# Sums of weight quarters in HBM: 32 transfers of 512 KB instead of 16 of 1 MB, from attention on

## The chip, the cores and the metric

The kernel runs on one core of a Trainium2 chip. TensorE does the matrix products, VectorE (DVE) and ScalarE (ACT) the elementwise work and the splitting of operands, GpSimd (POOL) a little arithmetic and the DMAs of its own queue, SyncE (SP) issues nearly all loads. The metric is the device time of one execution in microseconds (us), lower is better. Runs of before: 1167.38, 1168.90 and 1169.53 us, median 1168.9.

## The reference: two layers of attention, convolution and SwiGLU

Input is 512 tokens of 1024 features, float32. Each of two layers does:

```python
h = rms_norm(x, pre_mix_norm[l])
proj = h @ w_in[l]                                # q | k | v | conv_u | gate_b | gate_c
attn = dilated_mixture_attention(rope(q), rope(k), v)       # 8 heads, three dilated windows
conv_y = gate_b * short_conv(gate_c * conv_u, conv_w[l])    # depthwise, width 3
merged = concat(rms_norm(attn), rms_norm(conv_y))
x = x + rms_norm(merged @ w_out[l], post_mix_norm[l])
h = rms_norm(x, pre_ffn_norm[l])
g, u = split(h @ w_gate_up[l])                    # 2 x 2816 columns
f = (silu(g) * u) @ w_down[l]                     # 2816 -> 1024
x = x + rms_norm(f, post_ffn_norm[l])
```

## The kernel before

**Operands in two parts.** Every float32 operand is split into a rounded high part and the rest, and a product is three matmuls: high x high, high x low, low x high (mm3, lines 250 to 252). ScalarE makes the high part (line 221 for a weight half of 128 x 1024, 820 in the seven-product stage), VectorE the low part (222, 821).

**Weights.** A layer's weights lie in HBM in chunks of 1 MB, two halves of 512 KB each. load_raw (line 122) loads a half into one of three buffers, raw; a load waits until VectorE has read the buffer's last contents. split_half asks for the next two halves before it splits one. SP issues all of this in program order, so a wait at one load holds whatever stands behind it. The order of TensorE and SP is that of the program (a manual schedule); that of the other engines is made by the scheduler, and GpSimd's sum instructions are kept in the program's order among themselves.

**A layer's stages, in TensorE's order.** (1) in_proj_attention: projections, with attention's steps and the rotary and convolution work advanced between them; advance() is called once per weight tile of eight, 66 times a layer. (2) out_proj. Meanwhile split_by_dma makes the high and low parts of the first gate/up chunk by DMA on GpSimd's queue: a load (line 233), a negated copy on ScalarE (234), an accumulating load on top of it (235). (3) feed_forward: the gate/up product in 22 chunks. Chunks 0 to 3 are done directly, three of them in two halves of the tokens. Chunks 4 to 21 (the loop on SEVEN) are done in Strassen's manner, seven products of quarters instead of eight, which needs sums of weight quarters; prepare() makes these on chip, one chunk ahead: line 837 reads the chunk's first raw half, 838 its second too, 840 and 845 make the rest. The matmuls stand at line 900, 84 a chunk, of 256 columns. Line 777 multiplies gate and up. (4) The down projection: again seven products of quarters (line 994), in the order of weight_source: product 0 takes a quarter of the down weights as it is, product 1 the sum t1, then t2, a quarter, t3, a quarter, t4. A product takes four halves of 512 KB. The rest of the rows goes directly (line 1056).

**The sums in memory.** t1 to t4 are sums of the down weights' quarters, 2 MB each, made by DMA within HBM into tsum, one tensor a layer. weight_sums(l) is a generator; each step issues one transfer on GpSimd's queue, and the feed-forward stage takes a step behind every seven-product chunk. Six rounds: t1 and t3 are copies of a quarter; t1 and t3 each get another quarter added (an accumulating DMA, which reads its destination too); t2 is a copy of t1, then gets a quarter added; t4 is a copy of t2, then gets one added. Before, a transfer is 2048 columns of 128 rows, 1 MB, so that there are 16 a layer, behind chunks 4 to 19; eight are plain and eight accumulate.

**The token.** What sets a transfer's time is a token: SP issues a DMA of one number into a small buffer (due, line 158), behind the loads that the program has issued so far; GpSimd copies it (seen, line 159), so it waits until the token has landed; the transfer (line 160) follows. In the seven-product stage the token stands behind the two loads that prepare() issued for the next chunk but one.

Of the kernel before, what the change touches and what calls it, by code (L numbers as in the profile page):

```python
# [36 lines left out]
KS = 8  # L37
# [45 lines left out]
def encoder(ctx: ExitStack, tc: tile.TileContext, x, xT, pos, mask, cols, rows, w, wd, out):  # L83
    nc = tc.nc
# [6 lines left out]
    def nm(base):  # L91
        uid[0] += 1
        return f"{base}_{uid[0]}"

    def big(shape, dt=F32):
        return sb.tile(shape, dt, tag="big", bufs=11, name=nm("big"))
# [10 lines left out]
    def small(n, dt=F32):  # L107
        return sb.tile([P, n], dt, tag="small", bufs=24, name=nm("small"))

    def bank(tag):  # L110
        return ps.tile([P, 512], F32, tag=tag, bufs={"acc": 4, "att": 3, "pv": 1}[tag], name=nm(tag))
# [15 lines left out]
    def down_quarter(l, g, f):  # L127

        c = (2 * g + f) * KS * 512
        return wd[l][:, c:c + KS * 512]  # L130
# [15 lines left out]
    def weight_sums(l):  # L146

        b11, b12, b21, b22 = (down_quarter(l, g, f) for g in range(2) for f in range(2))  # L150
        t1, t2, t3, t4 = (tsum[l][:, k, :] for k in range(4))
        for pairs in (((t1, b11), (t3, b12)), ((t1, b12), (t3, b22)), ((t2, t1),), ((t2, b22),), ((t4, t2),), ((t4, b21),)):
            for n, (o, src) in enumerate(pairs):
                for c in range(0, KS * 512, 2048):
                    add = {"accum_op": ALU.add} if src is b22 or src is b21 or (src is b12 and o is t1) else {}
                    due = small(1)[:1]
                    seen = sb.tile([1, 1], F32, tag="seen", bufs=2, name=nm("seen"))
                    nc.sync.dma_start(due, cols[0:1, 0, 0:1])
                    tc.keep_in_program_order(nc.gpsimd.tensor_copy(seen, due))
                    tc.keep_in_program_order(nc.gpsimd.dma_start(o[:, c:c + 2048], src[:, c:c + 2048], **add))  # L160
                    yield

    tc.keep_in_program_order(nc.scalar.preload_act_table_set("trig_and_small"))
# [74 lines left out]
    def take(n, h, keep=None):  # L238


        return take_half(2 * n + h, keep)
# [7 lines left out]
    def mm3(o, sh, sl, mh, ml, start, stop):  # L249
        nc.tensor.matmul(o, sh, mh, start=start, stop=False)  # L250
        nc.tensor.matmul(o, sh, ml, start=False, stop=False)  # L251
        nc.tensor.matmul(o, sl, mh, start=False, stop=stop)  # L252
# [44 lines left out]
    def transposed(t, h, hT, tag, raw=None):  # L297
        for g in range(2):
            b = bank(tag)
            for k in range(4):  # L300
                nc.tensor.transpose(b[:, k * P:(k + 1) * P], h[:, (4 * g + k) * P:(4 * g + k + 1) * P], ident)
            b4 = b.rearrange("p (k t) -> p k t", k=4)
            hi = hT[0][g][:, :, t * P:(t + 1) * P]
            lo = hT[1][g][:, :, t * P:(t + 1) * P]
            nc.scalar.copy(hi, b4)
            nc.vector.tensor_sub(lo, b4, hi.bitcast(F32))
            if raw is not None:
                nc.scalar.copy(raw[g][:, :, t * P:(t + 1) * P], b4)
# [12 lines left out]
    def pair_full(n, hT, step=None, tag="acc"):  # L321
        accs = [bank(tag), bank(tag)]
        pair_part(n, accs, hT, 0, S, step)
        return accs
# [121 lines left out]
    def run_background(n=None):  # L446

        while background and n != 0:
            try:
                next(background[0])  # L450
                n = None if n is None else n - 1
            except StopIteration:
                background.pop(0)
# [143 lines left out]
                nc.scalar.activation(V[:, t, :], accs[t], AF.Copy, scale=inv[:, 2 * t:2 * t + 1])  # L597
        return inv

    def in_proj_attention(l, hT, h, tables):  # L600

        base = l * NCHUNK
        V = big([P, NT, S])
        accs = [None] * NT

        def values(t, g, turn=None):
            if accs[t] is None:
                accs[t] = bank("acc")
            for kt in range(4 * g, 4 * g + 4):
                if turn is not None and kt == 4 + TURN // 2:  # L610
                    transposed(turn, h[turn], hT, "acc")
                hi, lo = take(base + g, (kt % 4) // 2, 2 * base if t < NT - 1 else None)
                c = (kt % 2) * 512
                mm3(accs[t], hT[0][g][:, kt % 4, t * P:(t + 1) * P], hT[1][g][:, kt % 4, t * P:(t + 1) * P],
                    hi[:, c:c + 512], lo[:, c:c + 512], kt == 0, kt == KT - 1)
            if g == 1:
                nc.scalar.copy(V[:, t, :], accs[t])

        inv = None
        if l == 0:  # L620
            inv = first_values(hT, V)
            nc.sync.dma_start(mask_sb, mask)
        else:
            for o in [(0, 0), (0, 1, 2), (1, 0), (1, 1, 3), (2, 0), (2, 1), (3, 0), (3, 1)]:
                values(*o)

        qks = [None] * 4
        merged = [None] * 4
        sq_a = sb.tile([P, S], F32, tag="sqa", bufs=1, name=nm("sqa"))
        sq_c = sb.tile([P, S], F32, tag="sqc", bufs=1, name=nm("sqc"))  # L630
        att = attention(l, qks, V, merged, sq_a)
        count = [0]

        def advance():
            for _ in range(PACE[count[0] % len(PACE)]):
                next(att, None)
            run_background(BG)
            count[0] += 1

        made = []  # L640
        for j in range(4):
            if j == 1:
                merged[0:2] = [big([P, 2, 2, S], F32R) for _ in range(2)]
            seen = [0]

            def step():
                seen[0] += 1
                if l == 0 and j == 0 and seen[0] == TURN_ROT:
                    made.extend(rotary_tables(*angles, inv))
                if j > 1 or (j == 1 and seen[0] > START):  # L650
                    advance()
                elif j == 1:
                    run_background(BG)

            accs = pair_full(base + 2 + j, hT, step, "att" if l == 0 and j == 0 else "acc")
            if l == 0 and j == 0:
                tables, scaled, inv2 = made
            qk = big([P, 4, S], F32R)
            kl = sb.tile([P, 2, S], F32R, tag="kl", bufs=2, name=nm("kl"))
            background.append(rope_split(accs, scaled if l == 0 else tables, qk, kl))  # L660
            qks[j] = (qk, kl)
        merged[2:4] = [big([P, 2, 2, S], F32R) for _ in range(2)]
        kinds = ["u", "c", "b"] * 4
        held = {}
        for n in range(6):
            accs = pair_full(base + 6 + n, hT, advance)
            for m in range(2):
                i, kind = divmod(2 * n + m, 3)
                kind = "ucb"[kind]
                if kind == "u":  # L670
                    t = sb.tile([P, S], F32, tag="u", bufs=1, name=nm("u"))
                    if l == 0:
                        nc.vector.tensor_mul(t, accs[m], inv2)
                    else:
                        nc.scalar.copy(t, accs[m])
                    held["u", i] = t
                else:
                    held[kind, i] = accs[m]
                if kind == "b":
                    background.append(conv_tile(i, held["u", i], held["b", i], held["c", i], merged, l, sq_c))  # L680
        for _ in att:
            pass
        run_background()
        return merged, sq_a, sq_c, tables, inv
# [58 lines left out]
    def feed_forward(l, hT, hs, raw, adding):  # L743
# [35 lines left out]
        def gated_full(m, accs):  # L779
            sg = tmp([P, S])  # L780
            nc.scalar.activation(sg, accs[0], AF.Silu)
            gated(m, sg, accs[1])
# [159 lines left out]
        for m in range(3):  # L942
            pair_part(base + m, accs[m], hT, HS, S, step, keep if m == 0 else None)
            gated_full(m, accs[m])
        ahead = None
        for m in range(3, SEVEN):
            n = [0]
# [29 lines left out]
        hT = None  # L977
        hs = [None] * NT
# [64 lines left out]
        for f in range(2):  # L1043
            if f == 1 and gnext is not None:
                hT = new_hT()
            for t in range(NT):
                for m in range(2 * KS, MT):
# [5 lines left out]
                    c = (j % 2) * 512  # L1053
# [17 lines left out]
    with tc.manual_schedule(engines={mybir.EngineType.PE, mybir.EngineType.SP}):  # L1071
        warm_up()
        hs = [None] * NT
        hT = new_hT()
        tables = None
        for l in range(DEPTH):
            adding = weight_sums(l)
            merged, sq_a, sq_c, tables, inv = in_proj_attention(l, hT, hs, tables)
            hT, hs, raw = out_proj(l, merged, sq_a, sq_c, inv)
            hT, hs = feed_forward(l, hT, hs, raw, adding)  # L1080

# [87 lines left out]
```

## Time and profile before

| what | value |
|---|---|
| runs, median | 1168.9 us (1167.38 to 1169.53) |
| profiled execution | 1170.38 us, span 1168.4 us |
| granted TensorE clock | 0.997 |
| seven-product stage, layer 0 / layer 1 | 284.98 to 468.69 / 865.02 to 1051.61 us |
| DMA share, 285 to 470 us / 30 to 230 us | 0.69 / 0.29 |
| sums' DMAs, issued | 292.1 to 450.1 and 872.0 to 1031.2 us |
| HBM traffic | 159.36 MB read, 35.65 MB written |

The page's groups give line, engine, operation, the tiles (out<-in), their shape, the count, busy time and the mean of one. A row of a timeline gives start and duration in us, the engine, the line, and in brackets how long the engine stood before it and what ended that. "Waits" sum such times by who waited for whom. The chain follows the work that ended last back to its releasers. TensorE's matmuls overlap, so that one's duration is longer than the distance from one start to the next. A DMA row on POOL or SP is the issue; its landing is given apart. Rows by stretch give the length, the busy times of TensorE, its weight loads, VectorE, ScalarE and GpSimd with their counts, the granted clock, the share of the DMA engines and GB/s.

### The profile page before, as it was taken

How to read it: one execution, taken by the hardware profiler on the slowest of the kernel's cores; microseconds unless marked ns; L12 is line 12 of the kernel's file. 1: busy time of each engine (PE TensorE's matmuls, PEld its weight loads, DVE VectorE, ACT ScalarE, POOL GpSimd, SP SyncE). 2: the span in 40 equal slices, each digit the busy share in tenths (PEclk: the TensorE clock that was granted, in tenths of full speed). 3: DMA queues.
4: the chain of work that ended last, by engine and by line, in shares of the span. 5: the costliest groups of instructions: out<-in, count | busy, mean ns of one | idle time of the engine just before them, and what ended most of it. 6: DMA issues, size and time to landing. Idle time of an engine off the chain costs nothing.

```text
span 1168.4 us, 18250 instructions
## 1 busy us (share of the span) xinstructions
PE 1148.5 (98%) x7008; PEld 1010.5 (86%) x7008; DVE 841.4 (72%) x1392; ACT 669.8 (57%) x1263; POOL 70.0 (6%) x127
## 2 busy tenths in 40 slices
PE   9999999999999999999999999999999999999997
PEld 8777778899999999888777777788999999998886
DVE  5798664776886778984757986448767777789844
ACT  7577544564655656663545775446545556567632
POOL 6000011000010000000000000110000011000000
PEclk9999999999999999999999999999999999999999
DMA  8221234222677777665223212441136776676641
GB/s 323 91 72 55 73 90 126 74 73 90 206 185 191 213 216 181 217 203 176 69 66 100 73 55 72 126 125 53 59 125 193 203 196 182 207 181 213 198 144 73
DMA packets 41911, 162.64 MB, mean 139 GB/s; under 512 B 4960, under 2 KB 4960, under 8 KB 37728
## 3 DMA queue, kind: packets, MB, share of 16 engines
q1 hardware_dynamic: 35344, 122.64, 32.8%
q0 software_dynamic: 5760, 37.75, 13.7%
q8 instruction: 55, 0.90, 0.3%
q10 hardware_dynamic: 720, 1.09, 0.3%
q14 instruction: 32, 0.26, 0.1%
HBM read 159.36 MB, written 35.65 MB: 167 GB/s over the span
## 4 chain that ended last, share of the span: by engine, by line
PE 44%; DVE 3%; DMA 2%; ACT 1%; issue 1%; DVEq 0%; ACTq 0%; SPq 0%
PE acc L900 7%; PE att L900 6%; PE acc L250 5%; PE acc L251 5%; PE acc L252 5%; PE acc L994 5%; PE att L994 2%; DMA raw<-in_w 2%; PE acc L1056 1%; PE pv L487 1%; PE att L480 1%; PE att L1056 1%; PE att L250 1%; PE att L252 1%; PE att L251 1%
## 5 line engine op out<-in xcount | busy, mean ns | idle before, releaser
L222 DVE TENSOR_TENSOR wl<-raw,wh 128x1024 fp32r<-128x1024 f32 x140 | 170.7, 1220 | 79.3 <-ACT wh L221 78.2
L900 PE MATMUL acc<-big,wh 128*128 128x256 f32 x1152 | 212.2, 283 | 0.0
L221 ACT CAST wh<-raw 128x1024 fp32r<-128x1024 f32 x140 | 146.9, 1051 | 108.8 <-PE acc L251 35.9
L900 PEld LDWEIGHTS acc<-big,wh 128*128 128x128 f32 x1152 | 179.8, 192 | 0.2
L900 PE MATMUL acc<-big,wl 128*128 128x256 f32 x576 | 163.7, 284 | 2.8 <-DVE wl L821 2.8
L900 PE MATMUL att<-big,wh 128*128 128x256 f32 x864 | 160.7, 283 | 0.2 <-ACT att L908 0.2
L250 PE MATMUL acc<-big,wh 128*128 128x512 f32 (+1 forms) x400 | 154.0, 385 | 0.0
L252 PE MATMUL acc<-big,wl 128*128 128x512 f32 (+1 forms) x400 | 149.5, 374 | 0.0
L251 PE MATMUL acc<-big,wh 128*128 128x512 f32 (+1 forms) x400 | 149.3, 373 | 0.0
L900 PEld LDWEIGHTS att<-big,wh 128*128 128x128 f32 x864 | 134.6, 192 | 0.5 <-ACT att L908 0.4
L900 PE MATMUL att<-big,wl 128*128 128x256 f32 x432 | 123.2, 285 | 0.4
L820 ACT CAST wh<-t 128x512 fp32r<-128x512 f32 x144 | 88.7, 619 | 45.8 <-PE att L900 30.7
L900 PEld LDWEIGHTS acc<-big,wl 128*128 128x128 f32 x576 | 110.5, 192 | 3.9 <-DVE wl L821 3.7
L821 DVE TENSOR_TENSOR wl<-t,wh 128x1024 fp32r<-128x1024 f32 x72 | 87.7, 1218 | 17.3 <-ACT wh L820 17.3
L994 PE MATMUL acc<-wh,big 128*128 128x512 f32 x320 | 99.5, 389 | 0.0
L820 ACT CAST wh<-raw 128x512 fp32r<-128x512 f32 x108 | 63.4, 619 | 47.0 <-PE acc L900 31.3
L252 PEld LDWEIGHTS acc<-big,wl 128*128 128x128 f32 x400 | 75.3, 188 | 13.9
L250 PEld LDWEIGHTS acc<-big,wh 128*128 128x128 f32 x400 | 75.4, 189 | 12.3 <-issue 0.8
L251 PEld LDWEIGHTS acc<-big,wh 128*128 128x128 f32 x400 | 75.6, 189 | 11.6
L900 PEld LDWEIGHTS att<-big,wl 128*128 128x128 f32 x432 | 82.8, 192 | 2.2 <-DVE wl L821 2.2
L821 DVE TENSOR_TENSOR wl<-raw,wh 128x512 fp32r<-128x512 f32 x72 | 68.5, 951 | 6.2 <-ACT wh L820 6.0
L994 PEld LDWEIGHTS acc<-wh,big 128*128 128x128 f32 x320 | 60.1, 188 | 12.4
(265 smaller groups left out, 2225.5 us busy)
## 6 DMA issues: line engine op xcount, KB each, us to landing
raw<-in_w SPq DMA_DIRECT2D x144, 512.0 KB
tsum<-in_wd POOLq DMA_DIRECT2D x24, 1024.0 KB, 8.1
raw<-in_wd SPq DMA_DIRECT2D x36, 512.0 KB
raw<-tsum SPq DMA_DIRECT2D x32, 512.0 KB
tsum<-tsum POOLq DMA_DIRECT2D x8, 1024.0 KB, 5.3
gain<-in_rows SPq DMA_DIRECT2D x7, 512.0 KB
big<-in_xT SPq DMA_DIRECT2D x8, 256.0 KB
raw<-in_w SPq DMA_DIRECT2D x8, 256.0 KB
```

The lines of the kernel that those rows point to most:

```text
L221: nc.scalar.copy(hi, raws[i])
L222: nc.vector.tensor_sub(lo, raws[i], hi.bitcast(F32))
L250: nc.tensor.matmul(o, sh, mh, start=start, stop=False)
L251: nc.tensor.matmul(o, sh, ml, start=False, stop=False)
L252: nc.tensor.matmul(o, sl, mh, start=False, stop=stop)
L480: nc.tensor.transpose(tp[:, k * P:(k + 1) * P], sm[:, k * P:(k + 1) * P], ident)
L487: nc.tensor.matmul(o[hd * 64:hd * 64 + 64, half * 256:half * 256 + 256], V[:, k, hc:hc + 64], PT[hd][:, k, :], start=k == 0, stop=k == NT - 1)
L820: nc.scalar.copy(hi[:, c:c + 512], src[:, c:c + 512])
L821: nc.vector.tensor_sub(lo[:, :n], src[:, :n], hi[:, :n].bitcast(F32))
L900: nc.tensor.matmul(o[:, :HS], sh[:, c], mh[:, k, :], start=start and k == 0 and n == 0, stop=k == 3 and n == 2, skip_group_check=True)
L994: nc.tensor.matmul(outs[i], sh[:, k, st], mh[:, c:c + 512], start=start and k == 0 and n == 0, stop=False, skip_group_check=True)
L1056: nc.tensor.matmul(accs[f][t], sh[:, t * P:(t + 1) * P], mh[:, c:c + 512], start=False, stop=m == MT - 1 and n == 2, skip_group_check=True)
```

## The change

A transfer of the sums is 1024 columns, 512 KB, so a layer has 32, in the same six rounds. The generator is handed to in_proj_attention too. There every sixth call of advance() takes a step (calls 6, 12, ... of 66: 11 steps); each of the first three gate/up chunks takes one behind its second half (3 steps); each seven-product chunk takes one as before (18 steps, 4 to 21). 11 + 3 + 18 = 32, so that none is left for the loop behind the stage. By kind: the plain copies are transfers 1 to 8, 17 to 20 and 25 to 28, the accumulating ones 9 to 16, 21 to 24 and 29 to 32.

```diff
@@ weight_sums @@
-                for c in range(0, KS * 512, 2048):
+                for c in range(0, KS * 512, 1024):
...
                     nc.sync.dma_start(due, cols[0:1, 0, 0:1])
                     tc.keep_in_program_order(nc.gpsimd.tensor_copy(seen, due))
-                    tc.keep_in_program_order(nc.gpsimd.dma_start(o[:, c:c + 2048], src[:, c:c + 2048], **add))
+                    tc.keep_in_program_order(nc.gpsimd.dma_start(o[:, c:c + 1024], src[:, c:c + 1024], **add))
                     yield
@@ in_proj_attention @@
-    def in_proj_attention(l, hT, h, tables):
+    def in_proj_attention(l, hT, h, tables, adding):
...
         def advance():
+            if count[0] % 6 == 5:
+                next(adding, None)
             for _ in range(PACE[count[0] % len(PACE)]):
                 next(att, None)
             run_background(BG)
@@ feed_forward @@
         for m in range(3):
             pair_part(base + m, accs[m], hT, HS, S, step, keep if m == 0 else None)
             gated_full(m, accs[m])
+            next(adding, None)
@@ encoder @@
-            merged, sq_a, sq_c, tables, inv = in_proj_attention(l, hT, hs, tables)
+            merged, sq_a, sq_c, tables, inv = in_proj_attention(l, hT, hs, tables, adding)
```

## The prediction, made before the result was known

> **What bounds the kernel now.** I read the page first, then the stretches where TensorE changes stage, then the gaps inside the stage that the sums share with the weight loads, then what those gaps wait for. The page says that TensorE is busy almost all the time, so only its own gaps can be won; and it lists the sums, which GpSimd's queue q0 issues (packets, MB, share of the 16 engines' span).
>
> ```profile
> PE 1148.5 (98%) x7008; PEld 1010.5 (86%) x7008; DVE 841.4 (72%) x1392; ACT 669.8 (57%) x1263; POOL 70.0 (6%) x127
> ...
> q0 software_dynamic: 5760, 37.75, 13.7%
> ...
> tsum<-in_wd POOLq DMA_DIRECT2D x24, 1024.0 KB, 8.1
> ```
>
> In before all 16 sums of a layer run in the seven-product stage (line 900). How long is that stage, and how long need it be? TensorE's timeline gives its first matmul and the first one of the down projection (line 994) for layer 0; the chain gives the start for layer 1, and its own step.
>
> ```profile
> 284.98 0.40 PE L900 MATMUL acc<-big,wh 128*128 128x256 f32 x2
> ...
> 468.69 0.40 PE L994 MATMUL acc<-wh,big 128*128 128x512 f32 x1
> ...
> 865.02 2.87 PE acc L900 x24
> ...
> 895.25 2.88 PE acc L900 x24
> 898.13 1.44 PE att L900 x12
> ...
> 1051.61 0.40 PE L994 MATMUL acc<-wh,big 128*128 128x512 f32 x1
> ```
>
> 24 matmuls take 2.88 us undisturbed, 0.12 us each. The code issues 18 chunks x 7 products x 12 matmuls = 1512, so 181.44 us. Layer 0 took 468.69 - 284.98 = 183.71 us, layer 1 took 1051.61 - 865.02 = 186.59 us: 2.27 and 5.15 us lost, **7.4 us** together. That is all that this stage can give back. The chain names the cause for one of the gaps: a weight load that lands late, then VectorE's work on it (838), then the low half of a split (821) that TensorE stands for.
>
> ```profile
> 994.76 6.37 DMA raw<-in_w
> ...
> 1001.22 0.69 DVE t L838
> ...
> 1004.31 1.15 DVE wl L821
> ```
>
> ```profile
> 1003.77 0.38 PE L900 MATMUL acc<-big,wl 128*128 128x256 f32 x1 [0.88 <-DVE wl L821]
> ```
>
> So the lateness is that of the loads. Is it due to the sums? VectorE's timeline answers, by line 837, the first operation that needs a chunk's first load: beside the plain copies that open the stage it waits for nothing, from the first accumulating sum on it does, and late in the stage by 3.57 us.
>
> ```profile
> 302.20 0.69 DVE L837 TENSOR_TENSOR t<-raw 128x512 f32<-128x512 f32 x1
> ...
> 342.91 0.69 DVE L837 TENSOR_TENSOR t<-raw 128x512 f32<-128x512 f32 x1 [0.43 <-DMA raw<-in_w]
> ...
> 999.99 0.69 DVE L837 TENSOR_TENSOR t<-raw 128x512 f32<-128x512 f32 x1 [3.57 <-DMA raw<-in_w]
> ```
>
> The waits of the stage put a sum on it, layer 0 and layer 1 (us, times, longest):
>
> ```profile
> DVE t L837 <- DMA raw<-in_w: 16.0, 10, 3.0
> ...
> DVE t L837 <- DMA raw<-in_w: 18.4, 9, 3.6
> ```
>
> The sums' own rows, asked for by stretch, agree. First the four plain copies of layer 0 (290 to 332 us), then the four accumulating ones behind them (330 to 372 us), and last the two 512 KB accumulating DMAs of line 235, the nearest thing in this trace to a sum of the new size (the landing time there is that of these and of two plain 512 KB loads).
>
> ```profile
> L160 POOL DMA_DIRECT2D tsum<-in_wd x4: 515/524/587, 292.1 to 323.2; - x4
> ...
> DMA to landing us min/median/max: 4.9/5.1/5.3
> ...
> L160 POOL DMA_DIRECT2D tsum<-in_wd x4: 826/837/855, 333.7 to 366.8; - x4
> ...
> DMA to landing us min/median/max: 8.0/8.2/8.8
> ...
> L235 POOL DMA_DIRECT2D big<-in_w x2: 877/884/891, 182.1 to 762.0; - x2
> ...
> DMA to landing us min/median/max: 4.1/5.0/6.2
> ```
>
> Plain 1 MB: 5.1 us. Accumulating 1 MB: 8.2 us, and VectorE is late. Beside a plain one (302 to 313 us) the row of that stretch, its length and then the busy times with TensorE first, shows no gap:
>
> ```profile
> 302.00:313.00 11.00, 11.00 (x94) 11.00 (x93) 8.99 (x13) 6.37 (x14) 1.03 (x3) 1.00 0.66 197
> ```
>
> VectorE's slack takes up the first late loads; TensorE's gaps come in the stage's second half.
>
> **The change in the seven-product stage.** TensorE's, ScalarE's and VectorE's orders stay as they are (but for one pair of neighbours on VectorE); what moves is DMA traffic, SP's tokens and GpSimd's issues. Each chunk now carries 512 KB of sum, not 1 MB, and all 18 chunks carry one. A sum's place within the chunk's 10.08 us (84 x 0.12) stays:
>
> ```profile
> 302.87 0.53 POOL L160 DMA_DIRECT2D tsum<-in_wd  x1
> ...
> 306.19 3.42 SPq L122 DMA_DIRECT2D raw<-in_w  x2
> ```
>
> The sum starts 3.3 us ahead of the next chunk's first load. A sum of 8.2 us overlaps that load for 4.9 us and makes it late; one of 5.1 us overlaps for 1.8 us and does not. For a 512 KB sum I bound the landing by half of 8.2 (4.1 us) and by 6.2, the slowest of the 512 KB row, and take 5.0, its median: overlap 1.7 us, so like the plain copies, no gap. **Term: -7.4 us, less 0.2** for small gaps that hang on VectorE's order alone (an estimate: two of 0.1 us). At 6.2 us the overlap is 2.9, 1.1 of the 3.1 us between no wait and the full one: a third of the loss, 2.6 us, would stay. The Trainium skill ("DMA: Bandwidth & Descriptors", section "Anatomy of one DMA") has a fixed part of about 2 us in every GpSimd DMA, which speaks against halving them: by it a half-size accumulating sum would take an estimated (8.2 - 2) / 2 + 2 = 5.1 us and the stage's gain would be the same, but the margin smaller than a plain halving gives. The 512 KB row's median, 5.0, agrees.
>
> **What moves into attention.** Eleven sums of 512 KB now start beside the projections and the convolution. The loads there are issued two halves ahead; in all of 30 to 290 us ScalarE's cast waited for a load once:
>
> ```profile
> ACT wh L221 <- DMA raw<-in_w: 0.7, 1, 0.7
> ```
>
> A load that is 2 us later costs nothing there. The sharper point is GpSimd's queue near the end of attention, where it also issues the split of the first gate/up chunk (lines 233 and 235), for which ScalarE waits in order (line 234). Before, from the last addition into sqa on:
>
> ```order
> L442 TENSOR_TENSOR sqa_364<-sqa_364,tmp_1670 128x512
> L233 DMA big_2007<-in_w 128x1024
> L442 TENSOR_TENSOR sqc_365<-sqc_365,tmp_1786 128x512
> L235 DMA big_2007<-in_w 128x1024
> L442 TENSOR_TENSOR sqc_365<-sqc_365,tmp_1834 128x512
> ```
>
> Now, the same stretch (seen is the token's copy, tsum the sum behind it):
>
> ```order
> L442 TENSOR_TENSOR sqa_364<-sqa_364,tmp_1710 128x512
> L159 COPY seen_1760<-small_1759 1x1
> L160 DMA tsum_66<-in_wd 128x1024
> L159 COPY seen_1821<-small_1820 1x1
> L160 DMA tsum_66<-in_wd 128x1024
> L233 DMA big_2062<-in_w 128x1024
> L442 TENSOR_TENSOR sqc_365<-sqc_365,tmp_1836 128x512
> L159 COPY seen_1876<-small_1875 1x1
> L160 DMA tsum_66<-in_wd 128x1024
> L235 DMA big_2062<-in_w 128x1024
> ```
>
> Two sums, each with a wait for its token, now stand ahead of the 233 load, and one ahead of 235. The second token (small_1820) follows on SP's queue the load that before issues at 169.49; a token took 3.3 us from issue to GpSimd's copy in the first sum of before.
>
> ```profile
> 167.94 0.59 POOL L233 DMA_DIRECT2D big<-in_w  x1
> ...
> 169.49 0.33 SPq L122 DMA_DIRECT2D raw<-in_w  x1
> ...
> 180.14 1.04 ACT L234 ACTIVATE big<-big 128x1024 fp32r<-128x1024 f32 x1
> 183.52 1.05 ACT L221 CAST wh<-raw 128x1024 fp32r<-128x1024 f32 x1 [2.34 <-issue]
> ...
> 288.67 0.33 SPq L158 DMA_DIRECT2D small<-in_cols  x1
> ...
> 292.01 0.18 POOL L159 COPY seen<-small 1x1 f32<-1x1 f32 x1 [96.28 <-DMA small<-in_cols]
> ```
>
> So line 233 issues at about 169.5 + 0.4 + 3.3 + 0.9 = 174.1 instead of 167.9 and lands 5.0 later, or up to 11.2 later behind the sum ahead of it: 179 to 185. ScalarE, at line 234 from 180.14, waits 0 to 5 us; it then has 2.34 us of idle time, and its next casts stand two halves (10.9 us) ahead of their use. **Term: 0**; if the load came over 8 us late, each us more would cost one in each layer.
>
> **The first gate/up chunks.** Three sums, in a stretch with little traffic. The third meets the loads for the second seven-product chunk, for which line 838 waits already; behind it VectorE idles 3.3 us for TensorE (line 777), which takes up a delay.
>
> ```profile
> DVE big L777 <- PE acc L252: 3.3, 1, 3.3
> ```
>
> **Term: 0**, bound 1 us in each layer.
>
> **Into the down projection.** The last two sums now fall into chunks 20 and 21, free before. On SP's queue at the stage's end, before:
>
> ```order
> L122 DMA raw_5110<-in_wd 128x1024
> L122 DMA raw_5144<-in_wd 128x1024
> L122 DMA raw_5190<-tsum_66 128x1024
> L184 DMA gain_5201<-in_rows 128x1024
> L184 DMA gain_5203<-in_rows 128x1024
> L122 DMA raw_5227<-tsum_66 128x1024
> ```
>
> and now:
>
> ```order
> L158 DMA small_5143<-in_cols 1x1
> L122 DMA raw_5185<-in_wd 128x1024
> L122 DMA raw_5219<-in_wd 128x1024
> L122 DMA raw_5265<-tsum_66 128x1024
> L158 DMA small_5272<-in_cols 1x1
> L184 DMA gain_5281<-in_rows 128x1024
> L184 DMA gain_5283<-in_rows 128x1024
> L122 DMA raw_5307<-tsum_66 128x1024
> ```
>
> The last token comes behind the first load of a stored sum, and its accumulating sum runs beside two gain rows (one in layer 1) and the next load, product 1's second half, for which ScalarE waits already:
>
> ```profile
> 476.79 1.05 ACT L221 CAST wh<-raw 128x1024 fp32r<-128x1024 f32 x1 [2.76 <-DMA raw<-tsum]
> ...
> 479.00 1.22 DVE L222 TENSOR_TENSOR wl<-raw,wh 128x1024 fp32r<-128x1024 f32 x1
> ...
> 1059.65 1.22 DVE L222 TENSOR_TENSOR wl<-raw,wh 128x1024 fp32r<-128x1024 f32 x1
> ...
> 1051.78 10.91 PE acc L994 x48
> ```
>
> 48 matmuls take 10.91 us; this half is needed after 60, 13.64 us into the stage: at 482.33 in layer 0, where its split is done at 480.22, and at 1065.25 in layer 1, done at 1060.87. Slack 2.1 and 4.4 us. The sum takes the DMA engines for 13.7% x 1168.4 / 37.75 = 4.2 us a MB, so 2.1 us, if accumulating costs no more than the mean; up to 5 if the load waits for all of it. **Term: +0.2 us** (0 to 2.9 in layer 0, 0 to 0.6 in layer 1).
>
> Sum: -7.4 + 0.2 + 0.2 = -7.0 us. The profiled execution took 1170.38 us (span 1168.4), which makes 1163.4; it lies 1.5 us above the median of the three runs, 1168.9, so against that **1161.9**.
>
> **The rivals.** (1) *The accumulating sums still collide.* Ten of the stage's 18 sums accumulate; if they land at 6.2 us, 2.6 us stay, and with 1.4 at the boundary (the middle of its 0 to 2.9) it is -7.4 + 2.6 + 1.4 = -3.4 us: 1165.5. For it: the 512 KB row reaches 6.2. Against it: its median is 5.0. 0.16. (2) *The loads are late by themselves*: they are issued when VectorE frees a buffer, and size decides nothing; 1168.9. For it: some gaps lie beside plain copies late in the stage. Against it: the first four chunks of both layers run without one at the same spacing. 0.10. (3) *The wait moves into the down projection*, and the time ends above before's. Place: product 1's second half. It decides from 2.1 us (layer 0) and 4.4 us (layer 1) of delay on; if the last sum held up that load by the 8.2 us of a large one, 6.1 + 3.8 = 9.9 us would be lost and 7.2 won, 2.7 more than before: 1171.6. For it: ScalarE waits there already. Against it: the sum has half the size. 0.08. A change that does nothing it says is not among these: the token and sum rows above show it done.
>
> **How the numbers follow.** My forecast has 0.66, with 1159.8 to 1164.0 of its own: all of 7.4 off the lowest of the three runs, 1167.4, less 0.2 for rounding, at one end, 2 us more left at the other. The range reaches over most of rival 1: 1159.8 to 1166.4; rivals 2 and 3 lie outside. A measurement of this kernel can tell 0.2%, 2.3 us, from no change. Faster than 1166.6: forecast and nearly all of rival 1, 0.80; within: rival 2 and the rest of rival 1, 0.12; slower: rival 3, 0.08.
>
> **What would show it.** In the profile after: first matmul of line 900 to first of line 994 in 181.4 to 182.0 us in both layers; the sums of line 160 landing in 4 to 6 us; line 837 waiting for loads under 3 us in total per layer in that stage (16.0 and 18.4 would mean rival 2). ScalarE's line 234 after 180 us without a gap in TensorE behind it. Line 221's wait for raw<-tsum up by no more than 3 us with no gap in line 994; a gap there is rival 3. Wrong, too, if attention, from 30 to 230 us, grew by over half a us.

## The result and the profile after

The changed kernel takes 1161.46 us (median of 4 runs, 1161.23 to 1163.17) against 1168.73 us before (4 runs, 1167.38 to 1169.53): a ratio of 0.9942, 95% interval 0.9925 to 0.9959, so 7.3 us faster. Forecast were 1161.9 us and 7.0 us. The profiled execution took 1161.23 us.

The page after has the same bytes on GpSimd's queue in more and smaller packets, and sums that land sooner:

```profile
PE 1142.6 (99%) x7008; PEld 1008.4 (87%) x7008; DVE 848.0 (73%) x1392; ACT 668.4 (58%) x1263; POOL 108.8 (9%) x191
...
q0 software_dynamic: 10368, 37.75, 15.1%
...
tsum<-in_wd POOLq DMA_DIRECT2D x48, 512.0 KB, 5.6
...
tsum<-tsum POOLq DMA_DIRECT2D x16, 512.0 KB, 3.9
```

TensorE's timeline after gives the ends of the seven-product stage (line 902 is the former 900, 997 the former 994):

```profile
284.73 0.40 PE L902 MATMUL acc<-big,wh 128*128 128x256 f32 x2
...
466.27 0.40 PE L997 MATMUL acc<-wh,big 128*128 128x512 f32 x1
...
860.74 0.40 PE L902 MATMUL acc<-big,wh 128*128 128x256 f32 x2
...
1042.28 0.40 PE L997 MATMUL acc<-wh,big 128*128 128x512 f32 x1
```

The stage takes 181.54 us in both layers, 0.10 more than the 1512 steps of 0.12 us. For before, the same view shows that layer 1 began a little ahead of the chain's piece that the prediction used:

```profile
864.85 0.40 PE L900 MATMUL acc<-big,wh 128*128 128x256 f32 x2
```

So that stage took 186.76 us, and the change won 2.17 us in layer 0 and 5.22 in layer 1. The spans differ by more, 1168.4 - 1159.1 = 9.3 us. Of the rest, 0.25 us lies ahead of layer 0's stage, and 1.70 between layer 0's down projection and layer 1's seven products. That piece is no work of the change: in before's profiled execution the granted clock (the column behind GpSimd's count) fell to a mean of 0.72 over six us, as layer 1 began, and in the other it did not. Apart from the two kernels with all sums in attention, the profiled executions of the experiments below show both lengths of this piece, from the first matmul of the down projection to that of layer 1's seven products: about 394.5 us without this fall (as in "Size alone") and 396.1 with it (as in "No sums").

```profile
590.00:596.00 6.00, 6.00 (x25) 4.96 (x24) 4.06 (x10) 3.28 (x9) 0.00 (x0) 0.72 0.18 69
```

```profile
587.00:593.00 6.00, 5.66 (x29) 4.88 (x30) 5.19 (x13) 3.18 (x9) 0.00 (x0) 1.00 0.25 86
```

VectorE's waits for loads in layer 0's stage after: the former line 837 has none left (16.0 us before), the former 838 has half of its 12.7.

```profile
DVE t L840 <- DMA raw<-in_w: 6.2, 9, 1.4
```

The four accumulating sums of t2 (345 to 385 us) land in 5.3 to 5.6 us, where 8.0 to 8.8 were shown for those of 1 MB:

```profile
L160 POOL DMA_DIRECT2D tsum<-in_wd x4: 657/841/855, 353.4 to 383.3; - x4
...
DMA to landing us min/median/max: 5.3/5.5/5.6
```

Those behind them take 5.5 to 6.9 us in layer 0, but the last sum, beside the down projection's loads, takes 8.4 (7.9 in layer 1), and sums in attention and behind the gate/up chunks take up to 9.6. So the prediction's sign of 4 to 6 us did not hold everywhere; TensorE's seven products have no gap all the same.

The three places outside the stage that the prediction priced at 0, 0 and 0.2 us were paid for in slack. GpSimd's queue in attention: line 233 is issued at 175.45, and ScalarE stands at line 234 for 7.08 us, then does two casts at once.

```profile
174.91 0.83 POOL L160 DMA_DIRECT2D tsum<-in_wd  x1 [0.22 <-issue]
175.45 0.90 POOL L233 DMA_DIRECT2D big<-in_w  x1
```

```profile
187.06 1.06 ACT L234 ACTIVATE big<-big 128x1024 fp32r<-128x1024 f32 x1 [7.08 <-DMA big<-in_w]
188.03 1.98 ACT L221 CAST wh<-raw 128x1024 fp32r<-128x1024 f32 x2
```

The first gate/up chunks: VectorE waits 4.99 us for the load beside the third sum (1.7 before), and the 3.3 us that it idled behind are down to 0.33.

```profile
282.38 0.69 DVE L840 TENSOR_TENSOR t<-raw,t 128x512 f32<-128x512 f32 x1 [4.99 <-DMA raw<-in_w]
...
284.54 0.69 DVE L779 TENSOR_TENSOR big<-acc,tmp 128x512 f32<-128x512 f32 x1 [0.33 <-PE acc L252]
```

And into the down projection: ScalarE's wait at product 1's second half grows from 2.76 to 3.20 us; the split is done at 476.62, needed at 466.27 + 13.64 = 479.91.

```profile
474.31 1.05 ACT L221 CAST wh<-raw 128x1024 fp32r<-128x1024 f32 x1 [3.20 <-DMA raw<-tsum]
```

```profile
475.39 1.23 DVE L222 TENSOR_TENSOR wl<-raw,wh 128x1024 fp32r<-128x1024 f32 x1 [1.28 <-ACT wh L221]
```

### The profile page after: what moved, and what is told of

Read it like the earlier page. It is cut to its first block, busy times and chain, and to the rows that moved or that the text cites. A ratio compares the mean times of both kernels' runs of the same rounds, so it can differ in the third digit from the quotient of the medians.

```text
span 1159.1 us, 18413 instructions
## 1 busy us (share of the span) xinstructions
PE 1142.6 (99%) x7008; PEld 1008.4 (87%) x7008; DVE 848.0 (73%) x1392; ACT 668.4 (58%) x1263; POOL 108.8 (9%) x191
## 4 chain that ended last, share of the span: by engine, by line
PE 47%; DVE 2%; ACT 1%; issue 1%; DVEq 0%
PE acc L902 9%; PE att L902 7%; PE acc L997 5%; PE acc L250 5%; PE acc L251 5%; PE acc L252 5%; PE att L997 2%; PE acc L1059 1%; PE pv L487 1%; PE att L480 1%; PE att L1059 1%; PE att L250 1%; PE att L252 1%; PE att L251 1%; PE att L463 1%
## 5 line engine op out<-in xcount | busy, mean ns | idle before, releaser
L159 POOL COPY seen<-small 1x1 f32<-1x1 f32 x64 | 30.1, 471 | 752.3 <-DMA small<-in_cols 752.3
L251 PEld LDWEIGHTS acc<-big,wh 128*128 128x128 f32 x400 | 75.6, 189 | 11.6
```

## The experiments

Each kernel differs from before or from the changed kernel by the lines shown. In the rows by stretch, 286 to 464 us lies within layer 0's seven-product stage, so that TensorE's busy time (behind the length, 178 us) shows whether it has gaps there. It does not show the whole loss: for before 0.62 us are missing here, where the stage lost 2.27.

```profile
286.00:464.00 178.00, 177.38 (x1466) 176.13 (x1466) 137.69 (x189) 105.81 (x229) 14.26 (x32) 1.00 0.70 196
```

### Size alone

Before, with halves of the size and two of them behind each chunk:

```diff
-                for c in range(0, KS * 512, 2048):
+                for c in range(0, KS * 512, 1024):
...
             seven(m, ys[m % 2], ahead)
             next(adding, None)
+            next(adding, None)
```

> Size alone: 32 transfers of 512 KB, two behind each of chunks 4 to 19, none in attention. My theory (what makes the loads late is the accumulating bytes beside them in each chunk, and each chunk has as many as in before): 1167.5 to 1170 us, seven-product stage again 2 and 5 us over 181.5. Rival (the size of the single transfer, or its 8 KB rows, holds up the loads): 1161 to 1163 us.

Measured: 1170.08 us (11 runs), ratio to before 1.0009, interval 0.9999 to 1.0019, so no gain, and 0.08 us above the range of the theory. Line 837 waits for 17.5 us in layer 0, about as before the change (16.0), and TensorE has its gaps; its stages take 184.23 and 185.56 us.

```profile
DVE t L837 <- DMA raw<-in_w: 17.5, 9, 3.1
```

```profile
286.00:464.00 178.00, 176.97 (x1463) 175.66 (x1462) 137.26 (x189) 105.20 (x227) 27.39 (x64) 1.00 0.71 196
```

Two small transfers a chunk, with the bytes of one large one, bring nothing.

### Plain copies in place of accumulating ones

The additions are left out; all 16 transfers of 1 MB stay where they were.

```diff
-                    add = {"accum_op": ALU.add} if src is b22 or src is b21 or (src is b12 and o is t1) else {}
+                    add = {}
```

> Before with all 16 sums as plain copies of 1 MB (the additions are left out, everything else stays). My theory (a plain 1 MB lands in 5 us, early enough for the next load): 1161 to 1162.5 us, line 837 waits under 3 us a layer. Rival 1 (1 MB is too large in itself): 1167 to 1169. Rival 2 (loads late by themselves): 1168 to 1169.

Measured: 1161.47 us, ratio 0.9939, interval 0.9925 to 0.9952. TensorE has no gap:

```profile
286.00:464.00 178.00, 178.00 (x1484) 177.94 (x1483) 142.84 (x192) 107.27 (x231) 13.78 (x32) 1.00 0.61 196
```

This row and before's have the same 196 GB/s, and the share of the DMA engines is 0.61 against 0.70. Line 837 waits for no load in layer 0. So it is neither 1 MB as a size by itself nor the loads by themselves; the accumulating is what costs. Rival 2 of the prediction falls here.

### No sums

The transfers and tokens are left out, and the down projection loads plain quarters in place of the stored sums:

```diff
-            src = (lambda: down_quarter(l, 0, 0), lambda: tsum[l][:, 0, :], lambda: tsum[l][:, 1, :],
-                   lambda: down_quarter(l, 1, 0), lambda: tsum[l][:, 2, :], lambda: down_quarter(l, 1, 1),
-                   lambda: tsum[l][:, 3, :])[p]()
+            src = down_quarter(l, p % 4 // 2, p % 2)
...
-            adding = weight_sums(l)
+            adding = iter(())
```

> No sums at all: the down projection loads plain quarters in place of the stored sums, the 16 transfers and tokens of a layer are left out. My theory (the change hides the sums wholly): 1161.0 to 1161.6 us, equal to the changed kernel within 0.3. If the sums still cost something in attention or at the down projection's start: 1159 to 1161. Rival 2 (loads late by themselves): 1167 to 1169.

Measured: 1160.86 us, ratio 0.9937, interval 0.9924 to 0.9949; its stages take 181.55 and 181.54 us. That lies below the theory's range, in that of its alternative. The changed kernel is 0.6 us above this, where the theory allowed 0.3. Its stages are as short, so by these medians the sums cost it 0.6 us elsewhere at most; the scatter of runs (1160.78 to 1162.63 here, 1161.23 to 1163.17 there) is larger, so whether they cost anything isn't shown.

### Spread alone

The changed kernel with transfers of 1 MB: 7 in attention, none behind the first gate/up chunks, 9 in the stage, one behind every other chunk. The lines that set the place:

```diff
-            if count[0] % 6 == 5:
+            if count[0] % 9 == 8:
...
             seven(m, ys[m % 2], ahead)
-            next(adding, None)
+            if m % 2 == 1:
+                next(adding, None)
```

> Spread alone: transfers of 1 MB, 7 in attention (every ninth advance), 9 in the seven-product chunks, one behind every other chunk (5, 7, ... 21); five of these nine accumulate. The stage carries as many bytes as in the changed kernel. Each transfer by itself, as the prediction reckoned (8.2 us of landing make the next chunk's load late and TensorE stands 0.5 to 1 us each time): 5 x 2 x 0.7 = 7 us of gaps at most, 1164 to 1168. If VectorE's slack takes up a single late load and gaps come only from several in a row: 1161.2 to 1162.5.

Measured: 1162.59 us (5 runs, 1160.95 to 1164.38), ratio 0.9946, interval 0.9934 to 0.9959; the stages take 181.55 us in both layers. Five accumulating transfers of 1 MB a layer stand in this stage and make no gap:

```profile
286.00:464.00 178.00, 178.00 (x1485) 177.94 (x1484) 142.69 (x192) 107.40 (x231) 8.64 (x16) 1.00 0.51 150
```

So the prediction's reckoning for a single transfer was not the whole of it: a late load alone is taken up. The last pair of kernels below asks what makes the difference.

### Long rows

The changed kernel with transfers of 64 rows of 8 KB, again 512 KB:

```diff
-                for c in range(0, KS * 512, 1024):
+                for r, c in ((r, c) for c in range(0, KS * 512, 2048) for r in (0, 64)):
```

> The changed kernel with transfers of 64 rows of 8 KB instead of 128 rows of 4 KB: 512 KB as before, the same places. My theory (bytes and time count): 1161.2 to 1162.3 us. Rival (the long rows take the DMA engines' turns from the loads): gaps come back in the accumulating chunks, 1163 to 1166.

Measured: 1163.29 us (4 runs, 1161.37 to 1163.77), ratio 0.9948, interval 0.9933 to 0.9963. The median lies in the rival's range, but its stages take 181.55 us in both layers, without a gap; what its profiled execution has more lies at the start of layer 1, where the granted clock fell (0.50 from 588 to 591 us). The median is 1 us above my theory's range, too. But the rival said gaps in the stage, and there are none, so it fails; the time alone would have misled.

### All sums in attention

Transfers of 1 MB at every fourth advance:

```diff
-            if count[0] % 6 == 5:
+            if count[0] % 4 == 3:
```

> All 16 transfers of 1 MB in attention, one at every fourth advance; none in the feed-forward stage. The seven-product stage runs in 181.5 us. Three transfers (two plain, one accumulating: 5 + 5 + 8 us) then stand ahead of line 233's load, so that ScalarE waits at line 234 for 9 to 12 us, where 7 was free in the changed kernel. My theory (beyond 8 us each us costs one in each layer): 1162 to 1169. Rival (ScalarE's place there is off the path): 1161.2 to 1161.8.

Measured: 1166.73 us (10 runs), ratio 0.9989, interval 0.9977 to 1.0000. ScalarE waits 12.04 us at line 234, and layer 0's seven-product stage begins 3.69 us later than in the changed kernel:

```profile
192.00 1.06 ACT L234 ACTIVATE big<-big 128x1024 fp32r<-128x1024 f32 x1 [12.04 <-DMA big<-in_w]
```

```profile
288.42 0.40 PE L902 MATMUL acc<-big,wh 128*128 128x256 f32 x2
```

Transfers of 512 KB at every second advance:

```diff
-            if count[0] % 6 == 5:
+            if count[0] % 2 == 1:
```

> All 32 transfers of 512 KB in attention, one at every second advance; none in the feed-forward stage. Six transfers (four plain of 3.9, two accumulating of 5.5 us: 27 us) stand ahead of line 233's load from 167.7 us on; ScalarE waits at line 234 for about 17 us. My theory: 8 to 10 us lost in each layer, 1177 to 1182. Rival (off the path): 1161.2 to 1162.

Measured: 1167.10 us (10 runs), ratio 0.9988, interval 0.9978 to 0.9998. The expected 17 us of waiting were wrong: transfers queued one right behind the other overlap, so that their landing times don't add (the six are issued from 168.0 to 177.1 us, and each lands 4.8 to 10.2 us behind its issue). ScalarE waits 9.38 us in layer 0, and the stage begins 1.27 us late:

```profile
189.57 1.06 ACT L234 ACTIVATE big<-big 128x1024 fp32r<-128x1024 f32 x1 [9.38 <-DMA big<-in_w]
```

```profile
286.00 0.40 PE L902 MATMUL acc<-big,wh 128*128 128x256 f32 x2
```

In both kernels TensorE falls behind the changed kernel only after this wait (by under 0.3 us ahead of it), and both have stages of 181.5 us. Wait less loss is 12.04 - 3.69 = 8.35 and 9.38 - 1.27 = 8.11 us. In layer 1 ScalarE waits 12.04 and 10.12 us, and counted from the first matmul of line 1059 in layer 0 the stage begins 4.87 and 2.81 us late. Of these 1.70 are the fall of the clock, which both profiled executions have, so that 8.87 and 9.01 us were free there. So some 8 to 9 us of waiting are free, and nearly all of each further one is lost. The changed kernel's 7.08 stand one us below that edge. The rows do not sum up to the medians: the profiled executions took 1169.72 and 1165.29 us, and for the second kernel, whose median is 1.8 us above its profiled execution, where that time lies isn't shown.

### Two sums behind the last chunk

The changed kernel with none behind chunk 20 and two behind 21 (the loop behind the stage issues the second):

```diff
-            next(adding, None)
+            if m != MT - 2:
+                next(adding, None)
```

> The changed kernel, but chunk 20 carries no sum and chunk 21 two, so that 1 MB of accumulating transfers runs beside the first loads of product 1. Slack in the changed kernel's trace for that product's second half: 3.3 us in layer 0 (split done at 476.62, needed at 479.91), 4.4 in layer 1. By the row of queue 0 a transfer takes 2.1 to 2.5 us of the DMA engines. My theory: no gap or under 0.5 us, 1161.2 to 1162.2. Rival 3 (this is the point that breaks first): 2 us or more in line 997 of layer 0, 1163 to 1166.

Measured: 1161.08 us, ratio 0.9936, interval 0.9921 to 0.9950; stages and down projection as in the changed kernel. It did not load the place that rival 3 names, though. GpSimd's copy of one token took 6.69 us there (2.90 at this place in the changed kernel, whose 64 copies have a median of 0.36), so both sums started at 474 us and later, when product 1's second half had been cast already (473.07):

```profile
467.56 6.69 POOL L159 COPY seen<-small 1x1 f32<-1x1 f32 x1 [22.67 <-DMA small<-in_cols]
474.19 0.54 POOL L160 DMA_DIRECT2D tsum<-in_wd  x1
474.72 0.70 POOL L159 COPY seen<-small 1x1 f32<-1x1 f32 x1
475.36 0.53 POOL L160 DMA_DIRECT2D tsum<-in_wd  x1
```

Two accumulating transfers beside the down projection's later loads cost nothing; what a heavier load at that one half would cost stays open.

### In a row, or every other chunk

Both kernels have eight accumulating transfers of 1 MB in the stage and the eight plain ones in attention (t2 and t4 are copied from quarters, so that they lack a term). One has its eight behind chunks 4 to 11, the other behind 5, 7, ... 19.

```diff
-        for pairs in (((t1, b11), (t3, b12)), ((t1, b12), (t3, b22)), ((t2, t1),), ((t2, b22),), ((t4, t2),), ((t4, b21),)):
+        for pairs in (((t1, b11), (t3, b12), (t2, b11), (t4, b12)), ((t1, b12), (t3, b22), (t2, b22), (t4, b21))):
...
-            if count[0] % 6 == 5:
+            if count[0] % 8 == 7:
```

> Eight accumulating transfers of 1 MB behind eight chunks in a row (4 to 11); the eight plain ones stand in attention and copy other quarters, so that t2 and t4 lack a term (that part of the sums is left out). Theory of the loop (the token waits for the loads, the sum for the token, the next loads run beside the sum; with an accumulating 1 MB that circle takes 11.06 us in before's trace, a chunk on TensorE 10.08, and VectorE has some 4 us of slack): the tokens drift by 8 x 1 us, TensorE stands 2 to 4 us in each layer, 1165 to 1169. Theory of the single transfer (each late load costs what it costs): the same time as the kernel with every other chunk.

> The same eight accumulating transfers of 1 MB, behind every other chunk (5, 7, ... 19). Theory of the loop: a chunk without a sum lets the loads catch up, no drift, no gap: 1161.0 to 1162. Theory of the single transfer: the same time as with eight chunks in a row.

Measured: in a row 1166.66 us (10 runs), ratio 0.9992, interval 0.9982 to 1.0002; every other chunk 1161.98 us (4 runs), ratio 0.9949, interval 0.9931 to 0.9967. Tokens (GpSimd's copies) of the kernel in a row, the first and the last of eight in layer 0, and TensorE's busy time:

```profile
291.59 0.30 POOL L159 COPY seen<-small 1x1 f32<-1x1 f32 x1 [95.74 <-DMA small<-in_cols]
...
368.48 0.29 POOL L159 COPY seen<-small 1x1 f32<-1x1 f32 x1 [9.43 <-DMA small<-in_cols]
```

```profile
286.00:464.00 178.00, 176.75 (x1465) 175.84 (x1465) 138.13 (x189) 105.85 (x229) 8.29 (x16) 1.00 0.54 148
```

(368.48 - 291.59) / 7 = 10.98 us from token to token, where TensorE needs 10.08 for a chunk. The kernel with every other chunk:

```profile
302.48 0.45 POOL L159 COPY seen<-small 1x1 f32<-1x1 f32 x1 [106.37 <-DMA small<-in_cols]
...
444.12 0.17 POOL L159 COPY seen<-small 1x1 f32<-1x1 f32 x1 [18.52 <-DMA small<-in_cols]
```

```profile
286.00:464.00 178.00, 178.00 (x1484) 177.94 (x1484) 141.04 (x192) 107.08 (x231) 8.26 (x16) 1.00 0.54 149
```

(444.12 - 302.48) / 7 = 20.23 us for two chunks of 20.16: no drift, and 181.55 us for each stage against 183.90 and 184.80 in a row. The stage carries the same transfers in both, so what an accumulating transfer costs hangs on what follows it: in a row the tokens drift, with a free chunk in between they don't. That is what the loop of loads, token, sum and next loads says.

Before's own tokens show the same. The first four accumulating transfers of layer 0 start behind the first of these rows, the next two plain ones behind the second:

```profile
333.18 0.17 POOL L159 COPY seen<-small 1x1 f32<-1x1 f32 x1 [9.50 <-DMA small<-in_cols]
...
377.41 0.17 POOL L159 COPY seen<-small 1x1 f32<-1x1 f32 x1 [9.80 <-DMA small<-in_cols]
...
396.82 0.17 POOL L159 COPY seen<-small 1x1 f32<-1x1 f32 x1 [9.43 <-DMA small<-in_cols]
```

(377.41 - 333.18) / 4 = 11.06 us a chunk beside accumulating transfers, (396.82 - 377.41) / 2 = 9.71 beside plain ones, where the loads catch up a little. TensorE runs without a gap from 333 to 377 us, so it is the loads that set this pace. In the changed kernel the first token of the stage and the last behind a chunk of seven products, 16 chunks later, show no drift, (453.67 - 292.02) / 16 = 10.10 us:

```profile
292.02 0.58 POOL L159 COPY seen<-small 1x1 f32<-1x1 f32 x1 [17.61 <-DMA small<-in_cols]
...
453.67 0.17 POOL L159 COPY seen<-small 1x1 f32<-1x1 f32 x1 [9.34 <-DMA small<-in_cols]
```

No run takes the token away. That it is the token which closes the loop is read from the code, and that the transfers and loads together simply need more than a chunk's time of the DMA engines is not ruled out (their mean share is 0.77 from 333 to 377 us).

## Why the prediction was right, point by point

**The bound.** 7.4 us of gaps were read off the stage, all due to late loads. The change won 2.17 + 5.22 = 7.39 us there, and the two stages' remainder, 0.1 us each, was forecast as 0.2 together. Right; but whatever cures the lateness wins all of it, so the number says nothing of the cure.

**The cause.** That the accumulating sums make the loads late was right: plain copies of the same size and places give the whole gain (1161.47 us). That they do so transfer by transfer was too simple. The prediction had each 8.2 us transfer overlap the next load by 4.9 us and cost by itself; five such transfers a layer, spread, cost nothing, and eight behind every other chunk cost nothing either. Shown is a drift: with 1 MB accumulating in every chunk one turn takes 11 us, so each chunk falls back by 0.9 us until VectorE's slack is gone and TensorE stands. The code closes this to a loop: the token lies behind the loads, the sum behind the token, the next loads run beside the sum. The drift is also why the gaps of before lie in the stage's second half, which the prediction saw and put down to slack alone: the token of 419.02 us is 419.02 - 292.01 - 12 x 10.08 = 6.05 us behind TensorE's pace, and the first idle time that TensorE's timeline marks in layer 0's stage follows.

```profile
419.02 0.17 POOL L159 COPY seen<-small 1x1 f32<-1x1 f32 x1 [9.86 <-DMA small<-in_cols]
```

```profile
421.88 0.39 PE L900 MATMUL acc<-big,wl 128*128 128x256 f32 x1 [0.46 <-DVE wl L821]
```

**The size.** The landing forecast for 512 KB, 5.0 us within 4.1 to 6.2, was measured at 5.3 to 5.6 for the sums of t2, but at up to 6.9 and, for the last, 8.4 us. By the prediction's price for a single landing the one of 6.9 us, beside the loads of the seven products, would have left a gap; it left none. The step that took the halving for the cure is the one that the runs correct: halving alone gives nothing (1170.08 us), spreading alone gives the gain (stages of 181.55 us). The change works because each chunk carries half of the bytes.

**Attention.** The term of 0 was right, the wait under it was not: 7.08 us at line 234, where 0 to 5 were said, since line 233 was issued at 175.45, 1.4 us later than worked out, and ScalarE was released 11.6 us behind that, where a landing of 5 to 11.2 was said. The edge of 8 us, with one us lost for each beyond, was close: 8.11 and 8.35 in layer 0, about 9 in layer 1. So the 0 stood by one us of slack, not by the wait that was worked out, and in part by luck.

**The gate/up chunks and the down projection.** Terms of 0 and 0.2 us; both 0 by TensorE's timeline (the down projection's first part, line 994 to 1056, takes 77.10 us after and 77.09 before in layer 0, 77.10 in both in layer 1). The first was close: of the 3.3 us of idle time behind line 777, 0.33 are left.

**The rivals.** The first (gaps stay) and the second (loads late by themselves) did not come; the third (the down projection) was not reached, and its edge was not found.

## What to carry to other kernels

A background transfer that is released by the loads that it then delays can form a loop with them: compare its period with the work's, chunk by chunk, and look for drift, rather than price one collision. Before a change moves transfers, find what each queue that they join also carries; here eight us of slack in an in-order ScalarE queue decided how much attention could take. Take bytes out of a crowded stage first, or leave free chunks between them; cutting them smaller in place did nothing.

## What the runs showed of the hardware

In the seven-product stage an accumulating transfer within HBM lands later than a plain one of its size (medians, 1 MB: 8.2 against 5.1 us; 512 KB: 5.5 against 3.9), and halving it takes away a third, not half. The Trainium skill ("DMA: Bandwidth & Descriptors", section "Anatomy of one DMA") has a fixed part of about 2 us, by which 5.1 was estimated; the 5.5 measured agree better with that than with a plain halving, 4.1.

In some executions the granted clock falls to half for 3.41 us as TensorE restarts at layer 1's begin, after 2.1 us without a matmul. The profiled execution of the kernel of plain copies had this (first row); that of the changed kernel, with the same 2.1 us of waiting, had not (second row):

```profile
588.42:591.83 3.41, 3.41 (x11) 2.63 (x10) 2.34 (x7) 2.70 (x8) 0.00 (x0) 0.50 0.20 74
```

```profile
588.42:591.83 3.41, 3.41 (x16) 2.79 (x16) 2.69 (x9) 2.76 (x9) 0.00 (x0) 1.00 0.09 36
```

Half of 3.41 us is 1.7, and that is what it costs: 319.07 against 317.37 us from the first matmul of line 1056 in layer 0 to that of the seven products in layer 1. Why an execution has it was not tried. Nor was it tried what held up GpSimd's copy of a single number for 2.90 and 6.69 us.
